# Eight gathered rows move from beside the last build to the end of the block loop

## The chip, the cores and the metric

The kernel runs on one core of one Trainium2 chip. The metric is the device time of one execution in microseconds (us), as the median of several runs. The core has five engines with their own instruction queues: PE (TensorE, matmuls), DVE (VectorE), ACT (ScalarE), POOL (GpSimd, which here issues gathers) and SP (SyncE, which here issues loads and stores). Sixteen DMA engines move the data.

## The reference, cut to what matters

One encoder layer over 512 tokens of width 1024. The part that the change touches is the feed-forward by experts (PEER): every token picks 128 of 16384 experts (8 heads, 16 each), each expert being one row of a table U and one row of a table V.

```
def one_chunk(xb):                       # 128 tokens
    ...                                  # top-k over sub-keys: idx, g  (128 experts per token)
    u = u_table[idx]
    hpre = jnp.einsum('td,ted->te', xb, u)
    act = g * jax.nn.gelu(hpre, approximate=False)
    return jnp.einsum('te,ted->td', act, v_table[idx])
...
h = layer_norm(DN_ALPHA * h + ffn + ple, ln2_g[i], ln2_b[i])
```

## The kernel before, in words

The 512 tokens are four chunks of 128. Attention, the first LayerNorm and the routing (which experts, with which weights) take the first 550 us or so. After that the experts are computed in two ways at once.

Chunk 0 is gathered. For each of its 128 picks k, `gather_u` (or `rows`, earlier on) fetches 128 rows of U, one for each token, by an indirect DMA that POOL issues (128x1024 floats, 512 KB), and DVE multiplies them with the tokens and sums (`hdot[:, k]`). After all 128, `gather_act` applies the activation, and then `gather_v` fetches the 128 rows of V for each k and DVE adds them, scaled, to `base[0]`, the sum for chunk 0. That makes 128 + 1 + 128 steps, which stand in the list `steps`.

Chunks 1 to 3 are dense. V is walked in 128 blocks of 128 experts; for each block PE multiplies a matrix of weights (`a_hi`, `a_lo`: the weights split in two parts) with the block (`hTh`/`hTl` or `whi`/`wlo`: V split in two parts) into six accumulators `acc`. The weights come from a matrix G (which expert has which routing weight for which token) times the activations `ge` of the blocks of U. G is built by `build_g` once for each of the chunks 3, 2 and 1, in that order, from one-hot matrices (`oh_i`, `oh_j` on DVE and ACT, products `tr` on PE, `g_st` out of PSUM by ACT) and kept in DRAM.

Beside these builds, under the names `pe_work`, `gate_and_leads` and `lead_block`, PE multiplies blocks of U with tokens ("leads", 108 of the 128 blocks; in the trace `mm<-whole,raw` or `hp<-whole,raw`, 16 records a block) and the results go through ACT into `ge`. `run` walks over the steps of a build and hands PE so much lead work for each (`run_pe`), and from the generator `own` it takes steps of gathered rows in proportion to a share. In the last build (chunk 1) `own` is `beside()`: it fetches the first `BESIDE` rows of U of chunk 0 and, 12 and 5 rows before its end, loads two blocks of V that it later splits (`cut`).

Then comes the loop over the 128 blocks of V (`for n, i in enumerate(order)`). In each pass DVE multiplies `gt` (G) with `ge`, splits the block (`hTl` or `wlo`) and splits the weights (`a_lo`); then some steps of chunk 0 follow: a counter `spent` grows with each pass, and `upto` says up to which step the list is worked off. The order on DVE and on SP inside the loop is that of the code; PE, ACT and POOL are ordered by the scheduler. Blocks 124 to 127 (`late`) are multiplied after the loop's last pass, accumulator by accumulator. The buffers `whi`/`wlo` are two deep, so a block there can be split only when PE is done with the block two places before.

Behind the loop stand, for each chunk, the sum with the accumulator (`fsum`), the second LayerNorm (`layer_norm`) and the store. Chunk 0 has no accumulator: it needs the last `gather_v` alone.

Of the kernel before, what the change touches and what calls it, by code (L numbers as in the profile page):

```python
# [36 lines left out]
LEAD = 108  # L37
# [4 lines left out]
PACE = 1.1  # L42
AHEAD = 14.0
LAG = 6.0
BESIDE = 26
PRE = BESIDE
OWN = 1.2
OWN_G = 0.7
OWN_G_LATE = 4.0
SEAM = 7.0  # L50
WAIT = 8.4
OWN_LATE = 10.0
LATE = 0.57
OT = 8
W_SCALE = 32768.0
G_SPLIT = 1.0
# [6 lines left out]
NO_GATHER = 1  # L63
# [16 lines left out]
def tile_encoder_layer(ctx: ExitStack, tc: tile.TileContext, A: dict, out: bass.AP):  # L80
# [995 lines left out]
    def run_pe(amount):  # L1076
        nonlocal due
        due += amount * PACE
        while due > 0:
            done = next(pe_work, 1e9)  # L1080
            due -= done
        if due < -1e6:
            due = 0.0
# [313 lines left out]
    pe_work = gate_and_leads()  # L1397
    own, own_due = None, 0.0

    def run(steps, share=0.0, n=2):  # L1400

        nonlocal own_due
        for amount in steps:
            send()
            if amount is None:
                for _ in range(n if own else 0):
                    run_pe(next(own, 0.0))
                continue
            run_pe(amount)
            own_due += amount * share  # L1410
            while own and own_due > 0:
                x = next(own, None)
                if x is None or not x:
                    own_due = -1e9
                    break
                run_pe(x)
                own_due -= x

    with tc.manual_schedule(engines={nc.vector.engine, nc.scalar.engine, nc.tensor.engine, nc.sync.engine,
# [29 lines left out]
        build = build_g(NGC, *held)  # L1449
# [1 line left out]
        run_pe(next(side))  # L1451
        own = side
        own_due = -OWN_G_LATE
        run(build, OWN_G)
        for x in own:
            run_pe(x)
        while parts:
# [88 lines left out]
    def expert_out(x, c, halves=(0, 1)):  # L1546
        n, ah, al, vh, vl = x
        cs = slice(c * 128, (c + 1) * 128)
        for i, (a, b) in enumerate(((ah, vh), (ah, vl), (al, vh))):
            for hf in halves:  # L1550
                nc.tensor.matmul(acc[c][hf], a[:, cs], b[:, hf * 512:(hf + 1) * 512],  # L1551
                                 start=(n == 0 and i == 0), stop=(n == 127 and i == 2))

    steps = list(gather_steps())
# [8 lines left out]
    with tc.manual_schedule(engines={nc.vector.engine, nc.sync.engine}):  # L1563
        for n, i in enumerate(order):
# [59 lines left out]
                expert_in(u)  # L1624
            if n >= NO_GATHER:
                spent += 1 if u else LATE
            upto = min(len(steps), PRE + math.ceil((len(steps) - PRE) * spent / (128 - (1 - LATE) * LEAD - 3 - NO_GATHER)))
            for f in steps[done:upto]:
                f()
            done = upto  # L1630
        for c in range(NDC):
            for hf in range(2):
                for x in late:
                    expert_out(x, c, (hf,))


    turned.clear()
# [100 lines left out]
```

## Time and profile before

| what | value |
|---|---|
| median of 3 runs | 1489.12 us (1486.78 to 1490.31) |
| the profiled execution, its own time | 1489.54 us |
| its span in the profile | 1487.8 us |
| PE busy | 1450.2 us, 97% of the span |
| DVE busy | 1268.5 us, 85% |
| ACT busy | 638.4 us, 43% |
| POOL busy | 570.7 us, 38% |
| mean DMA rate over the span | 305 GB/s |

The span is what the profile covers; the execution's own time has 1.7 us more around it. Busy time counts the instructions on an engine alone. Times in the views below are in us from the span's start. In a row of the timeline stand the start, the length, the engine, the line of the kernel, what is written and read, and in brackets how long the engine had waited and for whom. The third build takes from about 810 to 880 us, the loop over V from 893 to 1477 us, and the last LayerNorms end at 1484 us.

### The profile page before, as it was taken

The page shows a single profiled execution, that of the slowest core. Times are in us where ns is not written, and L with a number is a line of the kernel's source. Part 1 is how long each engine was busy: PE and PEld are TensorE (multiplying, and loading weights), DVE is VectorE, ACT ScalarE, POOL GpSimd, SP SyncE. Part 2 cuts the span into 40 slices and gives each one's busy share as a digit, 9 for nine tenths or more (in the row PEclk, how much of TensorE's full clock was granted, in tenths as well). Part 3 has the DMA queues.
Part 4 walks back from the last instruction along what each step waited for, and adds up shares of the span by engine and source line. Part 5 has one row for each costly group of instructions (what it writes and reads, how often), then busy time and mean ns, then how long its engine had stood idle before and what let it go on. Part 6 is the DMA issues. An engine that isn't in the chain of part 4 may idle for free.

```text
span 1487.8 us, 22518 instructions
## 1 busy us (share of the span) xinstructions
PE 1450.2 (97%) x7693; PEld 1212.4 (81%) x7693; DVE 1268.5 (85%) x2736; ACT 638.4 (43%) x1203; POOL 570.7 (38%) x520
## 2 busy tenths in 40 slices
PE   9999999999999999999998999999999999999997
PEld 5788777788888878888887888988888888888775
DVE  7376786579998979998776987999899999999997
ACT  3355776243221554212555763444343333333433
POOL 1013110010014544344442435665555666666630
PEclk9999999999999999999999999999999999999999
DMA  7333340175239999999999999999999999999992
GB/s 255 99 111 92 97 128 30 29 245 170 100 125 351 334 416 415 405 324 336 392 416 410 376 396 369 415 417 417 401 393 411 412 412 411 412 412 412 411 362 85
DMA packets 196851, 453.82 MB, mean 305 GB/s; under 512 B 18945, under 2 KB 96897, under 8 KB 196738
## 3 DMA queue, kind: packets, MB, share of 16 engines
q1 hardware_dynamic: 119168, 211.72, 38.6%
q0 software_dynamic: 57984, 207.12, 35.5%
q10 hardware_dynamic: 19586, 33.57, 5.9%
q8 instruction: 60, 0.98, 0.2%
q14 instruction: 53, 0.43, 0.1%
HBM read 411.70 MB, written 37.75 MB: 302 GB/s over the span
## 4 chain that ended last, share of the span: by engine, by line
PE 56%; DMA 22%; DVE 9%; issue 6%; ACT 4%; POOL 3%; SPq 0%; ACTq 0%; DVEq 0%; POOLq 0%
PE acc L1551 16%; DMA raw<-in_v_rows_dram 11%; PE mm L1291 6%; PE hp L1291 5%; DMA ge_dram<-ge 4%; PE mm L129 4%; PE mm L131 4%; PE mm L130 4%; PE pj L129 3%; PE pj L130 3%; PE pj L131 3%; DMA v_raw<-in_v_rows_dram 3%; PE hp L129 1%; PE hp L131 1%; PE hp L130 1%
## 5 line engine op out<-in xcount | busy, mean ns | idle before, releaser
L110 DVE TENSOR_TENSOR wlo<-raw,whi 128x1024 fp32r<-128x1024 f32 (+4 forms) x113 | 131.5, 1164 | 45.7 <-ACT whi L110 45.4
L110 ACT CAST a_hi<-gt 128x384 fp32r<-128x384 f32 (+2 forms) x128 | 64.9, 509 | 242.4 <-DVE gt L1598 179.5
L110 ACT CAST whi<-raw 128x1024 fp32r<-128x1024 f32 (+4 forms) x113 | 113.0, 1001 | 106.9 <-PE mm L130 47.3
L1291 PE MATMUL mm<-whole,raw 128*128 128x256 f32 x672 | 153.1, 381 | 1.5 <-DMA raw<-in_uT_dram 1.5
L1174 POOL DMA_INDIRECT whi<-in_u_rows_dram,s_ix x51 | 64.2, 1259 | 218.5 <-DVE cand L994 129.7
L1551 PE MATMUL acc<-hTh,a_hi 128*128 128x512 f32 x456 | 141.8, 391 | 0.1
L1551 PE MATMUL acc<-hTl,a_hi 128*128 128x512 f32 x456 | 141.2, 390 | 0.0
L1551 PE MATMUL acc<-hTh,a_lo 128*128 128x512 f32 x456 | 140.9, 389 | 0.0
L1291 PEld LDWEIGHTS mm<-whole,raw 128*128 128x128 f32 x672 | 125.6, 190 | 17.9 <-DMA raw<-in_uT_dram 1.9
L1534 POOL DMA_INDIRECT gat<-in_v_rows_dram,i_sel x64 | 100.8, 1574 | 55.0 <-DVE base L1536 39.5
L110 ACT CAST hTh<-v_raw 128x1024 fp32r<-128x1024 f32 x74 | 77.8, 1051 | 55.9 <-PE acc L1551 23.1
L1551 PEld LDWEIGHTS acc<-hTl,a_hi 128*128 128x128 f32 x456 | 85.4, 188 | 18.3 <-DVE hTl L110 0.4
L1551 PEld LDWEIGHTS acc<-hTh,a_lo 128*128 128x128 f32 x456 | 85.4, 188 | 18.2 <-DVE a_lo L110 0.3
L1551 PEld LDWEIGHTS acc<-hTh,a_hi 128*128 128x128 f32 x456 | 84.1, 188 | 17.2 <-ACT a_hi L110 1.1
L110 DVE TENSOR_TENSOR hTl<-v_raw,hTh 128x1024 fp32r<-128x1024 f32 x74 | 90.2, 1219 | 6.4 <-ACT hTh L110 6.4
L1551 PE MATMUL acc<-wlo,a_hi 128*128 128x512 f32 x300 | 92.8, 390 | 0.2
L1551 PE MATMUL acc<-whi,a_hi 128*128 128x512 f32 x300 | 92.8, 391 | 0.1
L1551 PE MATMUL acc<-whi,a_lo 128*128 128x512 f32 x300 | 92.6, 390 | 0.0
L1174 POOL DMA_INDIRECT wlo<-in_u_rows_dram,s_ix x51 | 61.9, 1213 | 68.3 <-DVE s_dot L1176 56.0
L1519 POOL DMA_INDIRECT gat<-in_u_rows_dram,i_sel x52 | 69.1, 1329 | 45.2 <-DVE hdot L1525 34.1
L1536 DVE SCALAR_TENSOR_TENSOR base<-gat,hdot,base 128x1024 f32<-128x1024 f32 x64 | 82.0, 1281 | 1.0
L1273 ACT ACTIVATE ge<-mm 128x256 f32<-128x256 f32 x78 | 29.6, 380 | 110.4 <-PE mm L1291 100.5
(415 smaller groups left out, 3815.7 us busy)
## 6 DMA issues: line engine op xcount, KB each, us to landing
raw<-in_uT_dram SPq DMA_DIRECT2D x80, 512.0 KB, 7.8
v_raw<-in_v_rows_dram SPq DMA_DIRECT2D x78, 512.0 KB, 13.2
raw<-in_v_rows_dram SPq DMA_DIRECT2D x48, 512.0 KB, 13.8
g_dram<-g_st ACTq DMA_DIRECT2D x40, 512.0 KB, 12.1
ge_dram<-ge ACTq DMA_DIRECT2D x96, 128.0 KB, 7.0
ge<-ge_dram SPq DMA_DIRECT2D x96, 128.0 KB, 13.0
gt<-g_dram SPq DMA_DIRECT2D x30, 384.0 KB, 13.9
raw_u<-in_uT_dram SPq DMA_DIRECT2D x19, 512.0 KB, 7.8
```

The lines of the kernel that those rows point to most:

```text
L110: cut = nc.scalar.copy(hi, src), nc.vector.tensor_tensor(lo, src, r32(hi), op=OP.subtract)
L129: nc.tensor.matmul(ps, a[0], b[0], start=start, stop=False)
L130: nc.tensor.matmul(ps, a[0], b[1], start=False, stop=False)
L131: nc.tensor.matmul(ps, a[1], b[0], start=False, stop=stop)
L1174: nc.gpsimd.indirect_dma_start(out=u[:], out_offset=None, in_=u_rows, in_offset=bass.IndirectOffsetOnAxis(ap=ix[:, k:k + 1], axis=0))
L1273: nc.scalar.activation(ge, ps[:, :N_U], AF.Gelu)
L1291: nc.tensor.matmul(ps[:, :N_U], raw[:, k], whole[:, k, :], start=(k == 0), stop=(k == 7))
L1519: nc.gpsimd.indirect_dma_start(out=u[:], out_offset=None, in_=u_rows, in_offset=bass.IndirectOffsetOnAxis(ap=i_sel[:, c, k:k + 1], axis=0))
L1534: nc.gpsimd.indirect_dma_start(out=u[:], out_offset=None, in_=v_rows, in_offset=bass.IndirectOffsetOnAxis(ap=i_sel[:, c, k:k + 1], axis=0))
L1536: nc.vector.scalar_tensor_tensor(base[c], u, hdot[:, c, k:k + 1], base[c], op0=OP.mult, op1=OP.add)
L1551: nc.tensor.matmul(acc[c][hf], a[:, cs], b[:, hf * 512:(hf + 1) * 512], start=(n == 0 and i == 0), stop=(n == 127 and i == 2))
```

## The change

`BESIDE` goes from 26 to 18: beside the last build stand 18 rows of U of chunk 0 in place of 26. The list of steps is the same, so the loop starts 8 steps further ahead in it. The pace of the loop is now worked out for all steps but the last 8 (`LAST_ROWS`), 231 steps as before; so a pass of the loop has as many rows as before, each 8 places earlier in the list, and the list is worked off but for 8 rows of V at n = 121, where before all of it was. Of those 8, one each goes into the passes n = 124 to 127, and four stand behind the loop. Two numbers for the last build change besides: the share of `own` steps (0.7 to 0.6) and 0.2 us of lead work more on PE for every step of the build (`MORE_G`).

```diff
-BESIDE = 26
+BESIDE = 18
 PRE = BESIDE
 OWN = 1.2
-OWN_G = 0.7
+OWN_G = 0.6
...
+MORE_G = 0.2
+LAST_ROWS = 8
...
-    def run(steps, share=0.0, n=2):
+    def run(steps, share=0.0, n=2, more=0.0):
...
-            run_pe(amount)
+            run_pe(amount + more)
...
-        run(build, OWN_G)
+        run(build, OWN_G, more=MORE_G)
...
-            upto = min(len(steps), PRE + math.ceil((len(steps) - PRE) * spent / (128 - (1 - LATE) * LEAD - 3 - NO_GATHER)))
+            upto = min(len(steps) - LAST_ROWS, PRE + math.ceil((len(steps) - LAST_ROWS - PRE) * spent / (128 - (1 - LATE) * LEAD - 3 - NO_GATHER)))
+            upto += max(0, n - 123)
             for f in steps[done:upto]:
                 f()
             done = upto
...
+        for f in steps[done:]:
+            f()
```

Lines of the changed kernel lie 2 further down up to the new lines in the loop and 5 further down behind them (L1536 is L1538 there, L1646 is L1651).

DVE at the end of the loop, before: the LayerNorm of chunk 0 (L138, L166 on `base`) lies among the splits of blocks 124 to 127, and behind the last split (`a_lo`) come the sums with the accumulators (L1646).

```order
L138 TENSOR_TENSOR ln_y<-ln_y 128x1
L166 SCALAR_TENSOR_TENSOR base_3028<-base_3028,ln_y,gat 128x1024
L110 TENSOR_TENSOR wlo<-v_raw,whi 128x1024
L110 TENSOR_TENSOR raw<-gt_13358,raw 128x384
L1598 TENSOR_TENSOR gt_13358<-gt_13358,ge 128x8x32
L110 TENSOR_TENSOR hTl<-v_raw,hTh 128x1024
L110 TENSOR_TENSOR a_lo<-gt_13358,a_hi 128x384
L1598 TENSOR_TENSOR gt_13358<-gt_13358,ge 128x8x32
L110 TENSOR_TENSOR hTl<-v_raw,hTh 128x1024
L110 TENSOR_TENSOR a_lo<-gt_13358,a_hi 128x384
L1646 SCALAR_TENSOR_TENSOR h_86,fsum<-acc_8458,own_top,h_86 128x512
L1646 SCALAR_TENSOR_TENSOR h_86,fsum<-acc_8459,own_top,h_86 128x512
```

The same place now, from the last split on: the last rows of V (L1538) stand between the sums with the accumulators (L1651), and the LayerNorm of chunk 0 begins behind them.

```order
L112 TENSOR_TENSOR hTl<-v_raw,hTh 128x1024
L112 TENSOR_TENSOR a_lo<-gt_13334,a_hi 128x384
L1538 SCALAR_TENSOR_TENSOR base_3028<-gat,hdot,base_3028 128x1024
L1651 SCALAR_TENSOR_TENSOR h_86,fsum<-acc_8434,own_top,h_86 128x512
L1538 SCALAR_TENSOR_TENSOR base_3028<-gat,hdot,base_3028 128x1024
L1651 SCALAR_TENSOR_TENSOR h_86,fsum<-acc_8435,own_top,h_86 128x512
L1538 SCALAR_TENSOR_TENSOR base_3028<-gat,hdot,base_3028 128x1024
L1651 SCALAR_TENSOR_TENSOR h_87,fsum<-acc_8436,h_87 128x512
L1538 SCALAR_TENSOR_TENSOR base_3028<-gat_w,hdot,base_3028 128x1024
L1651 SCALAR_TENSOR_TENSOR h_87,fsum<-acc_8437,h_87 128x512
L1538 SCALAR_TENSOR_TENSOR base_3028<-gat_w,hdot,base_3028 128x1024
L150 BN_STATS ln_st<-base_3028 128x6 x2
```

So five rows of V moved behind the last split (that of n = 127 and the four behind the loop), and chunk 0's LayerNorm moved behind all of them.

PE between the last product of the third build and the loop's first matmul (`acc`), before: 33 lead matmuls, of which the last 16 go to the PSUM tile `hp`.

```order
L1291 MATMUL mm<-whole,raw 128x256
L1291 MATMUL mm<-whole,raw_u 128x256 x8
L1291 MATMUL mm<-whole,raw 128x256 x8
L1291 MATMUL hp<-whole,raw 128x256 x16
L1551 MATMUL acc_8460<-hTh,a_hi 128x512
```

The same place now: 17 lead matmuls, 8 of them to `hp`.

```order
L1117 LDWEIGHTS oh_j
L1117 MATMUL tr<-oh_i,oh_j 128x128
L1293 MATMUL mm<-whole,raw 128x256 x9
L1293 MATMUL hp<-whole,raw 128x256 x8
L1553 MATMUL acc_8436<-hTh,a_hi 128x512
```

So 16 of the 33 lead matmuls moved from behind the build in between its products.

ACT at the same seam, before: the last `ge` out of a PSUM tile `mm` stands ahead of `whi`, the first part of the block n = 2 of V, which needs that block's load.

```order
L110 CAST hTh<-h_s 128x1024
L110 CAST a_hi<-gt_7619 128x256
L1473 COPY gt_8567<-g_st 128x256 x2
L1273 ACTIVATE ge<-mm 128x256
L110 CAST a_hi<-gt_7619 128x256
L110 CAST a_hi<-gt_7619 128x128 x2
L110 CAST whi<-v_raw 128x1024
L1273 ACTIVATE ge<-hp 128x256 x2
```

And now:

```order
L112 CAST hTh<-h_s 128x1024
L112 CAST a_hi<-gt_7619 128x128 x2
L1475 COPY gt_8543<-g_st 128x256 x2
L112 CAST whi<-v_raw 128x1024
L1275 ACTIVATE ge<-mm 128x256
L1275 ACTIVATE ge<-hp 128x256
```

The last `ge<-mm` moved behind `whi<-v_raw`.

## The prediction

> **What bounds the kernel now.** I read the table of stretches first, because the change takes work out of one stretch (the third build) and puts it into another (the end of the loop), and a share over the whole span says nothing about either. Its columns are the busy time of PE, PE's weight loads, DVE, ACT and POOL, then the granted PE clock and the DMA share.
>
> ```profile
> 815.00:828.00 13.00, 10.16 (x81) 8.68 (x81) 12.90 (x20) 11.66 (x31) 3.73 (x3) 1.00 0.82 297
> 828.00:893.40 65.40, 62.57 (x433) 55.29 (x433) 56.13 (x91) 45.20 (x110) 23.81 (x20) 0.97 1.02 403
> 893.40:1436.00 542.60, 542.37 (x2612) 456.48 (x2611) 517.26 (x693) 211.12 (x303) 333.03 (x226) 1.00 1.03 408
> 1436.00:1461.00 25.00, 24.85 (x105) 18.77 (x104) 22.91 (x36) 11.73 (x17) 0.00 (x0) 1.00 0.56 202
> 1461.00:1468.30 7.30, 7.30 (x31) 5.28 (x30) 5.57 (x8) 2.93 (x5) 0.00 (x0) 1.00 0.23 93
> 1468.30:1477.60 9.30, 9.26 (x41) 7.32 (x39) 7.83 (x24) 2.89 (x6) 0.00 (x0) 1.00 0.09 35
> 1477.60:1487.80 10.20, 0.00 (x0) 0.00 (x0) 6.01 (x19) 1.45 (x3) 0.00 (x0) 0.74 0.30 122
> ```
>
> From the third build to its last matmul the kernel lives on PE: in the loop PE is busy 542.37 of 542.60 us. DVE and the DMA engines are nearly full there too, but PE never waits for them. The number of lead matmuls and products does not change, so an earlier start of the loop can come from one source only: time that PE idles, or runs at a low clock, before it. Behind PE's last matmul 10.2 us remain, and they belong to DVE and to the last store. The end of the chain of waits (start, length, engine, what) shows the hand-over:
>
> ```profile
> 1443.46 24.82 PE acc L1551 x103
> 1468.31 2.04 DVE h L1646 x6
> ...
> 1482.54 1.28 DVE h L166
> ```
>
> DVE's last instruction ends at 1483.82; the span ends 4.0 us later, with the last store. Whatever DVE has to do more at the end shows in full, as soon as it lies behind PE.
>
> **Term 1, the build: what 8 rows fewer are worth.** Taken out are 8 indirect DMAs of 512 KB on POOL's queue and 8 multiply-and-sum instructions on DVE. Neither is on PE, so the gain is what PE waits less. First SP's issues ahead of 828, then PE's waits in the build (in brackets), with an undisturbed product (855.94) and an undisturbed pair of lead blocks (886.58) for comparison:
>
> ```profile
> 819.76 0.38 SPq L1447 DMA_DIRECT2D gt<-g_dram  x1
> 820.23 1.07 SPq L1251 DMA_DIRECT2D raw<-in_uT_dram  x2
> ```
>
> ```profile
> 827.99 1.56 PE L1291 MATMUL mm<-whole,raw 128*128 128x256 f32 x6 [1.46 <-DMA raw<-in_uT_dram]
> ...
> 855.94 1.08 PE L1115 MATMUL tr<-oh_i,oh_j 128*128 128x128 f16 x16
> 856.85 1.08 PE L1291 MATMUL mm<-whole,raw_u 128*128 128x256 f32 x4
> 859.04 1.11 PE L1115 MATMUL tr<-oh_i,oh_j 128*128 128x128 f16 x16 [1.11 <-ACT g_st L1128]
> 861.87 1.86 PE L1115 MATMUL tr<-oh_i,oh_j 128*128 128x128 f16 x16 [1.72 <-ACT g_st L1128]
> 863.53 2.05 PE L1291 MATMUL mm<-whole,raw_u 128*128 128x256 f32 x6
> ...
> 886.58 7.07 PE L1291 MATMUL hp<-whole,raw 128*128 128x256 f32 x32
> 893.29 0.81 PE L1551 MATMUL acc<-hTh,a_hi 128*128 128x512 f32 x2
> ```
>
> Up to 828 I expect no gain. PE stands there for the load of a block of U, issued at 820.23 behind a load that waited for G in DRAM. In the changed order PE has the same 27 lead matmuls and the same 3 products behind it when it needs that block, and SP's loads ahead of it have not moved: PE arrives earlier and waits longer. The 2.84 us of idle time in the stretch before (13.00 less 10.16) stay.
>
> From 828 to 893.40 PE idles 65.40 - 62.57 = 2.83 us, which is the two waits of 1.11 and 1.72. The clock of 0.97 costs another 0.03 x 65.4 = 2.0 us; one sees it in the product at 861.87, which takes 1.66 us up to the next row where the one at 855.94 takes 0.91. So 4.8 us is the most there is to win. Those two waits come where two products follow each other with hardly any lead work between (the code holds 7 us of leads back for the seam, `SEAM`), and ACT is late with `g_st`. In the changed order this place exists as well, with 5 lead matmuls ahead of the pair and 3 behind, and ACT has as much to do. But elsewhere a product now has about 8 lead matmuls with it (each is two records; 16 records are 3.36 us by the row at 886.58, which has 32 in 6.71), so DVE and ACT, with fewer rows to share with, come to the pair with more of a lead. I take half of 4.8, rounded: **-2.5 us**. The ends: all of it (-4.8), or a loss of 1.5 if the seam opens (rival C).
>
> The 16 lead matmuls that moved ahead cost nothing in themselves; what hides the seam is the 17 that are left, about 17 x 2 x 0.21 = 7.1 us.
>
> **Term 2, the loop up to n = 121.** The pace is the same 231 steps over the same passes, so POOL issues and DVE works as much per pass as before; eight rows of U stand there in place of eight of V. Both engines keep their slack against PE (517.26 of 542.60 on DVE). Zero, and the cover is PE; if PE started more than a few microseconds ahead of the loads, DMA at 1.03 would be late next.
>
> **Term 3, the end: eight rows of V more on DVE.** A row of V takes 1.19 us from its start to the next instruction's. The rows that matter on DVE at the end, and the matmuls that hold it:
>
> ```profile
> 1434.85 1.28 DVE L1536 SCALAR_TENSOR_TENSOR base<-gat,hdot,base 128x1024 f32<-128x1024 f32 x1
> 1436.04 0.41 DVE L1598 TENSOR_TENSOR gt<-gt,ge 128x256 f32<-128x256 f32 x1
> ...
> 1451.38 0.69 DVE L148 BATCH_NORM_STATS2 ln_st<-base 128x6 f32<-128x512 f32 x1
> ...
> 1453.91 0.69 DVE L148 BATCH_NORM_STATS2 ln_st<-base 128x6 f32<-128x512 f32 x1
> 1454.64 0.21 DVE L149 BATCH_NORM_AGGREGATE ln_mu<-ln_st 128x2 f32<-128x12 f32 x1
> ...
> 1454.95 1.27 DVE L163 SCALAR_TENSOR_TENSOR base<-base,ln_mu,gat 128x1024 f32<-128x1024 f32 x1
> ...
> 1459.60 1.29 DVE L166 SCALAR_TENSOR_TENSOR base<-base,ln_y,gat 128x1024 f32<-128x1024 f32 x1
> 1461.98 1.23 DVE L110 TENSOR_TENSOR wlo<-v_raw,whi 128x1024 fp32r<-128x1024 f32 x1 [1.09 <-ACT whi L110]
> ...
> 1468.31 0.75 DVE L1646 SCALAR_TENSOR_TENSOR h<-acc,own_top,h 128x512 f32<-128x512 f32 x1 [0.75 <-PE acc L1551]
> ...
> 1471.97 0.15 DVE L158 TENSOR_SCALAR ln_y<-ln_y 128x1 f32<-128x1 f32 x1 [1.36 <-ACT gat_w L157]
> ```
>
> ```profile
> 1460.11 0.62 PE L1551 MATMUL acc<-whi,a_lo 128*128 128x512 f32 x2
> ...
> 1477.17 0.39 PE L1551 MATMUL acc<-hTh,a_lo 128*128 128x512 f32 x1
> ```
>
> ```profile
> 1459.95 1.05 ACT L110 CAST hTh<-v_raw 128x1024 fp32r<-128x1024 f32 x1
> 1460.90 1.05 ACT L110 CAST whi<-v_raw 128x1024 fp32r<-128x1024 f32 x1
> ```
>
> The anchor is 1461.98: DVE's split of block 125. It cannot come earlier against PE, since ACT's `whi` takes the buffer that PE frees with the last matmul of block 123 (1460.11). Before the change, LayerNorm of chunk 0 fills DVE's time in front of that anchor. Now it cannot, since `base` still lacks seven rows at this point: the row of n = 124 fits in, and then DVE waits some 4 us with nothing to do (4.3 for that LayerNorm, worked out below, plus the 1.09 it waits today, less 1.19). All the rest comes behind the anchor:
>
> - seven rows of V (n = 125, 126, 127 and the four): 7 x 1.19 = 8.3 us;
> - LayerNorm of chunk 0: 0.69 + 0.69 + 0.21 + 1.27 + 1.29 = 4.2 us and seven instructions of about 0.15 on one column, less some 0.08 of overlap each: 4.3 us;
> - less what DVE idles behind the anchor today and can fill: 0.75 + 1.36 = 2.1 us, and a little between the dependent small steps of the last LayerNorms, about 0.2.
>
> 8.3 + 4.3 - 2.3 = **+10.3 us**, from 1483.82 to about 1494. PE ends at 1477.6 and does not cover it: in DVE's order the six sums with the accumulators stand between the last rows and behind them. The store behind it keeps its 4.0 us. The ends: 9 (more small gaps filled) and 11.5 (waits for the activations of ACT in the tail, which now come close to each other). The gathers themselves are hidden: their buffers are freed at the latest by the row that is the last today, and a gather lands within about 8 us:
>
> ```profile
> 1448.72 1.28 DVE L1536 SCALAR_TENSOR_TENSOR base<-gat_w,hdot,base 128x1024 f32<-128x1024 f32 x1
> ```
>
> ```profile
> gat<-in_v_rows_dram,i_sel POOLq DMA_INDIRECT x64, 8.1
> ```
>
> **Sum.** 1489.5 - 2.5 + 0 + 10.3 = 1497.3 us against the profiled execution; the median of the runs shown lies 0.4 lower, so 1497 (+0.5%). Two runs differ by up to 0.2% (1486.78 to 1490.31), about what a measurement of this kernel can tell from no change.
>
> **Rivals.**
>
> A, faster: the eight rows cost nothing at the end, since DVE gets through them while PE still multiplies 16.6 us (1460.6 to 1477.2). Then only term 1 is left: 1489 - 2.5 to -4.8, about 1485.5. For it: DVE is idle there at times. Against it: it would need 12.6 us of idle DVE time behind the anchor to take the seven rows and the LayerNorm, and there are 2.3; it decides in the moment that DVE finishes the fourth row before 1470. Chance 0.05.
>
> B, no change: the build is held by the DMA engines and not by ACT. They are at 1.02 there with 403 GB/s; 8 x 524,288 bytes are 4.2 MB, or 10.4 us at that rate, more than everything PE loses. Then all waits go, the ones ahead of 828 too: 2.84 + 4.8 = 7.6, and 1489.1 - 7.6 + 10.3 = 1491.8. For it: ACT's own queue waits for its stores in this stage. Against it: the wait at 828 is for a load that is issued late, at a DMA share of 0.82. [...] Chance 0.09.
>
> C, slower still: the seam opens. The first `acc` matmul takes the PSUM tile that the last `ge<-mm` frees, and this now stands behind `whi<-v_raw` in ACT's order.
>
> ```profile
> 880.54 1.52 SPq L1489 DMA_DIRECT2D v_raw<-in_v_rows_dram  x3
> ...
> 890.92 1.05 ACT L110 CAST whi<-v_raw 128x1024 fp32r<-128x1024 f32 x1 [2.18 <-DMA v_raw<-in_v_rows_dram]
> ```
>
> The block landed 10.4 us after its issue; `whi` and `ge` take 1.4 more, and PE has 7.1 us of leads behind the last product. If the load is issued when the last product ends, PE waits 10.4 + 1.4 - 7.1 = 4.7 us. But the load now waits for DVE's last row only, which DVE can reach some 4 us before PE's last product, so I expect a wait of 0 to 1. With 4.7 lost and 2.5 won, the time is 1489.1 + 2.2 + 10.3 = 1501.6. A pause of this length has a second price, which the trace shows at 861.87, where 2.8 us of waits bring the clock to 0.97 over the stretch. [...] Chance 0.18.
>
> That the change does not do what it says is excluded by the order of the instructions.
>
> **How the numbers follow.** The forecast as summed has 0.68, C 0.18, B 0.09, A 0.05. The likeliest gives 1497, with its own range from 1493.3 (9 - 4.8) to 1500 (11.5, -0.5). Out to 1501.5 it takes in C; down to 1492.5 the edge towards B. Slower by over 0.2% (above 1492.1): the forecast and C, 0.86. Within 0.2%: B, 0.09. Faster: A, 0.05.
>
> **What the profile afterwards would show.** Right: DVE waits 3 to 5 us ahead of block 125's split, then is busy without a gap for 32 us, the LayerNorm of chunk 0 lies behind PE's last matmul, and from that matmul to the end of the span are about 20 us in place of 10.2. The first `acc` comes at 889 to 892 in place of 893.3, and PE stands at about 828 longer than 1.46. Wrong: `acc` earlier than 888 (B), or `base` normalised before the last matmul (A), or a wait of the first `acc` for ACT (C).

## The result, and the profile after

| | median | runs |
|---|---|---|
| before | 1487.95 us | 6 (1486.19 to 1493.84) |
| after | 1497.07 us | 6 (1495.71 to 1498.07) |

The ratio is 1.0055, with a 95% interval from 1.0037 to 1.0074: slower by about half a per cent. The profiled execution of the changed kernel took 1496.71 us, with a span of 1494.7; the one of before took 1489.54 with 1487.8.

Four instants cut the span into stages: the starts of PE's first transposition of the third build (`tr<-ident,e1s`), of the first `acc` and of the last `acc`, and the end of DVE's last instruction. Their rows in the timeline (start, length, engine); first the one of before that the prediction has not shown, then those of after:

```profile
809.75 0.27 PE L1090 MATMUL tr<-ident,e1s 128*128 128x128 f32 x1
```

```profile
811.26 0.27 PE L1092 MATMUL tr<-ident,e1s 128*128 128x128 f32 x1
890.97 0.81 PE L1553 MATMUL acc<-hTh,a_hi 128*128 128x512 f32 x2
1474.34 0.39 PE L1553 MATMUL acc<-hTh,a_lo 128*128 128x512 f32 x1
1489.50 1.28 DVE L168 SCALAR_TENSOR_TENSOR h<-h,ln_y,gat 128x1024 f32<-128x1024 f32 x1
```

| stage | before | after | difference |
|---|---|---|---|
| up to the third build | 809.75 | 811.26 | +1.51 |
| build, to the first `acc` | 83.54 | 79.71 | -3.83 |
| loop, to the last `acc` | 583.88 | 583.37 | -0.51 |
| tail, to DVE's end | 6.65 | 16.44 | +9.79 |
| last store | 3.98 | 3.92 | -0.06 |
| span | 1487.8 | 1494.7 | +6.9 |

So the tail costs 9.8 us, and the build wins some of it back. The 1.51 us ahead of the build lie where the change touches nothing; in the profiles of the experiments below that instant lay anywhere from 808.36 to 811.73, so it is what two executions differ by.

The stretches of after, cut at the matching places (busy time of PE, PE's weight loads, DVE, ACT, POOL; then the granted clock, the DMA share and GB/s):

```profile
815.00:828.00 13.00, 13.00 (x95) 11.24 (x95) 11.65 (x19) 10.35 (x26) 2.30 (x2) 1.00 0.86 319
828.00:891.00 63.00, 60.81 (x427) 53.81 (x425) 47.61 (x77) 46.45 (x113) 15.61 (x13) 0.97 0.89 342
891.00:1433.70 542.70, 542.70 (x2619) 458.44 (x2618) 517.98 (x703) 210.45 (x303) 337.45 (x229) 1.00 1.03 409
1433.70:1458.20 24.50, 23.19 (x99) 17.45 (x98) 19.07 (x24) 10.49 (x15) 8.09 (x5) 1.00 0.86 328
1465.50:1474.70 9.20, 9.20 (x41) 7.21 (x39) 9.20 (x16) 1.80 (x2) 0.00 (x0) 1.00 0.32 114
1474.70:1494.70 20.00, 0.03 (x1) 0.00 (x0) 15.87 (x46) 4.32 (x10) 0.00 (x0) 0.62 0.26 105
```

Behind PE's last matmul lie 20.0 us in place of 10.2, and DVE is busy in 15.87 of them. From 1465.5 to 1474.7 DVE is busy all the time (9.20 of 9.20), where before it had gaps.

The tail on DVE, in order (in brackets the wait and for whom):

```profile
1454.52 0.41 DVE L1600 TENSOR_TENSOR gt<-gt,ge 128x256 f32<-128x256 f32 x1
1459.25 1.23 DVE L112 TENSOR_TENSOR wlo<-v_raw,whi 128x1024 fp32r<-128x1024 f32 x1 [4.33 <-ACT whi L112]
1460.40 0.55 DVE L112 TENSOR_TENSOR raw<-gt,raw 128x384 fp32r<-128x384 f32 x1
1460.87 1.28 DVE L1538 SCALAR_TENSOR_TENSOR base<-gat_v,hdot,base 128x1024 f32<-128x1024 f32 x1
...
1467.14 1.28 DVE L1538 SCALAR_TENSOR_TENSOR base<-gat,hdot,base 128x1024 f32<-128x1024 f32 x1
1468.33 0.74 DVE L1651 SCALAR_TENSOR_TENSOR h<-acc,own_top,h 128x512 f32<-128x512 f32 x1
...
1474.49 1.27 DVE L1538 SCALAR_TENSOR_TENSOR base<-gat_w,hdot,base 128x1024 f32<-128x1024 f32 x1
1475.79 1.29 DVE L150 BATCH_NORM_STATS2 ln_st<-base 128x6 f32<-128x512 f32 x2
```

DVE waits 4.33 us ahead of the split of block 125, and then works off seven rows, the sums and four LayerNorms. The LayerNorm of chunk 0 begins at 1475.79, behind PE's last matmul. From that split to DVE's end it is 1490.78 - 1459.25 = 31.53 us; before, it was 1483.82 - 1461.98 = 21.84.

PE in the build has one wait left in this execution, at two products with no lead work in between, and the clock is low there (0.50 from 841.3 to 844.7; 16 products take 1.66 us up to the next row, where the undisturbed ones of the prediction's rows take 0.91):

```profile
838.25 1.08 PE L1117 MATMUL tr<-oh_i,oh_j 128*128 128x128 f16 x16
841.52 1.86 PE L1117 MATMUL tr<-oh_i,oh_j 128*128 128x128 f16 x16 [2.19 <-ACT g_st L1130]
843.18 1.16 PE L1293 MATMUL mm<-whole,raw_u 128*128 128x256 f32 x2
```

### The profile page after: what moved, and what is told of

Same layout as the page of the kernel before. It is cut to its first block, busy times and chain, and to the rows that moved or that the text cites. A ratio compares the mean times of both kernels' runs of the same rounds, so it can differ in the third digit from the quotient of the medians.

```text
span 1494.7 us, 22522 instructions
## 1 busy us (share of the span) xinstructions
PE 1451.2 (97%) x7693; PEld 1215.7 (81%) x7693; DVE 1268.5 (85%) x2736; ACT 638.7 (43%) x1203; POOL 570.6 (38%) x520
## 4 chain that ended last, share of the span: by engine, by line
PE 74%; DMA 10%; DVE 8%; ACT 3%; issue 3%; POOL 1%; ACTq 0%; DVEq 0%; POOLq 0%; SPq 0%
PE acc L1553 28%; PE mm L1293 10%; PE hp L1293 5%; DMA ge_dram<-ge 5%; PE mm L131 4%; PE mm L133 4%; PE mm L132 4%; DMA ge<-ge_dram 4%; PE pj L131 3%; PE pj L132 3%; PE pj L133 3%; PE tr L1117 2%; PE hp L131 1%; PE hp L133 1%; PE hp L132 1%
## 5 line engine op out<-in xcount | busy, mean ns | idle before, releaser
L1293 PE MATMUL mm<-whole,raw 128*128 128x256 f32 x688 | 156.6, 381 | 0.0
L1293 PEld LDWEIGHTS mm<-whole,raw 128*128 128x128 f32 x688 | 129.1, 191 | 17.0 <-DMA raw<-in_uT_dram 0.3
L1536 POOL DMA_INDIRECT gat<-in_v_rows_dram,i_sel x64 | 101.9, 1593 | 59.7 <-DVE base L1538 45.1
L1521 POOL DMA_INDIRECT gat<-in_u_rows_dram,i_sel x56 | 74.4, 1329 | 51.0 <-DVE hdot L1527 40.6
L1538 DVE SCALAR_TENSOR_TENSOR base<-gat,hdot,base 128x1024 f32<-128x1024 f32 x64 | 81.9, 1280 | 0.9
L112 DVE TENSOR_TENSOR a_lo<-gt,a_hi 128x384 fp32r<-128x384 f32 (+2 forms) x128 | 69.6, 544 | 10.3 <-ACT a_hi L112 9.9
## 6 DMA issues: line engine op xcount, KB each, us to landing
g_dram<-g_st ACTq DMA_DIRECT2D x40, 512.0 KB, 12.6
```

Of the source, the lines that this page charges most:

```text
L112: cut = nc.scalar.copy(hi, src), nc.vector.tensor_tensor(lo, src, r32(hi), op=OP.subtract)
L1293: nc.tensor.matmul(ps[:, :N_U], raw[:, k], whole[:, k, :], start=(k == 0), stop=(k == 7))
L1521: nc.gpsimd.indirect_dma_start(out=u[:], out_offset=None, in_=u_rows, in_offset=bass.IndirectOffsetOnAxis(ap=i_sel[:, c, k:k + 1], axis=0))
L1536: nc.gpsimd.indirect_dma_start(out=u[:], out_offset=None, in_=v_rows, in_offset=bass.IndirectOffsetOnAxis(ap=i_sel[:, c, k:k + 1], axis=0))
L1538: nc.vector.scalar_tensor_tensor(base[c], u, hdot[:, c, k:k + 1], base[c], op0=OP.mult, op1=OP.add)
```

## The experiments

Every kernel is told by its difference from the changed kernel. The medians of the kernel before differed a little from one set of runs to the next (1487.95 to 1489.99 us), so each ratio is against the runs of before in the same set. The stages come from one profiled execution of each kernel, cut at the four instants above:

| kernel | median, us | ratio to before (95%) | build | loop | tail |
|---|---|---|---|---|---|
| before | | | 83.54 | 583.88 | 6.65 |
| after | 1497.07 | 1.0055 (1.0037 to 1.0074) | 79.71 | 583.37 | 16.44 |
| e1 build only | 1494.76 | 1.0049 (1.0036 to 1.0062) | 80.01 | 592.41 | 6.63 |
| e2 end only | 1495.75 | 1.0048 (1.0032 to 1.0065) | 81.25 | 580.64 | 16.38 |
| e3 held rows sooner | 1490.83 | 1.0011 (0.9999 to 1.0023) | 80.47 | 586.08 | 7.85 |
| e4 fewer rows only | 1501.06 | 1.0085 (1.0072 to 1.0098) | 86.80 | 584.41 | 16.40 |
| e6 leads only | 1491.95 | 1.0026 (1.0012 to 1.0040) | 79.50 | 590.42 | 6.64 |
| e7 eight not gathered | 1488.14 | 0.9989 (0.9977 to 1.0000) | 81.23 | 584.31 | 6.64 |
| e8 eight not added | 1495.19 | 1.0038 (1.0023 to 1.0054) | 81.04 | 591.77 | 6.63 |
| e9 leads, three held | 1492.89 | 1.0025 (1.0015 to 1.0035) | 79.68 | 589.27 | 6.64 |
| e10 leads and share | 1491.67 | 1.0012 (1.0000 to 1.0024) | 82.46 | 583.68 | 6.62 |
| e11 two rows more | 1487.29 | 0.9985 (0.9973 to 0.9997) | 84.14 | 580.65 | 6.65 |
| e12 last four out | 1491.22 | 1.0014 (1.0001 to 1.0026) | 81.93 | 583.58 | 11.64 |
| e13 seam seven | 1485.45 | 0.9975 (0.9963 to 0.9987) | 79.58 | 581.20 | 6.63 |

The table also says how far one execution can be trusted. The build of after, e1, e3, e7, e8 and e12 is in the same order of code and took 79.7 to 81.9 us; that of before and e2 took 83.5 and 81.3. A difference of 2 us in the build of one execution is not yet an effect. The tail repeats within 0.1 us (6.62 to 6.65; 16.38 to 16.44). Nor is a profiled execution always a middle one: that of e4 took 2.9 us more than the median of its kernel and that of e12 2.3 more, that of e10 2.8 less.

### The two halves apart (e1, e2)

```diff
 e1: the rows are spread over the pace of the loop
-LAST_ROWS = 8
+LAST_ROWS = 0
...
-            upto += max(0, n - 123)
```

> The half of the change at the build alone: 18 rows of U beside the third build with 0.6 and 0.2 as in the changed kernel, but no row held back; the eight rows are spread over the loop's pace up to n = 121 (239 steps in place of 231), and the end is as in the kernel before. Theory (the build gives 2 to 4 us, the tail on DVE costs all the rest, and the loop hides rows under PE, since DVE was busy 517.26 of 542.60 us there and eight rows are 9.5): first acc at 889 to 891.5, PE without a wait in the loop, DVE's end about 6 us behind PE's last matmul as before, 1485.5 us (1484.5 to 1487). Rival (the loop has no room either, because its DMA share is 1.03 at 408 GB/s, and eight gathers more before n = 121 are 4.2 MB or 10.3 us at that rate): PE waits in the loop for its blocks or for DVE's splits, 1490 to 1496 us.

The theory on the loop fell here, and the time lies in the rival's range. The tail came as expected and the first `acc` at 888.37, 0.6 us ahead of the range, but the loop took 8.5 us more: 1494.76 us, about as slow as the whole change.

```diff
 e2: the build as before
-BESIDE = 18
+BESIDE = 26
-OWN_G = 0.6
+OWN_G = 0.7
-MORE_G = 0.2
+MORE_G = 0.0
```

> The half of the change at the end alone: 26 rows beside the build with 0.7 and 0.0 as before, and the last eight rows of V held back as in the changed kernel (the loop's pace is then 223 steps). Theory: first acc at 893 as before, DVE's wait of about 4 us ahead of block 125's split, 31.5 us from that split to DVE's end in place of 21.8, so +9.7 and no gain: 1497.6 us (1496.5 to 1499). If the two halves add up, this run less the kernel before and the build half less the kernel before together give the 9.1 us of the whole change. Rival (the slower pace gives the loop time back, DMA at 1.03 there): PE's last matmul 3 us or more sooner than the start of the loop explains, 1490 to 1494 us.

The tail costs 9.73 us, as expected. But the rival's mechanism is there as well: the loop, with 223 steps in place of 231, took 3.2 us less, and the median of 1495.75 lies between the two ranges. Set side by side, the places at which the six accumulators pass from one block to the next run apart between before and e2 at two places above all: by 1.6 us at 475 to 490 us into the loop, and by 1.1 at 545 to 557. The matmuls of the kernel before start a little later there one by one. PE's busy share does not show it, but the waits of PE's weight loads (PEld) do. In before, from 900 to 1450 (what waited for whom: us in total, times, longest):

```profile
PEld acc L1551 <- ACT a_hi L110: 2.2, 5, 0.5
PEld acc L1551 <- DVE wlo L110: 1.7, 5, 0.6
PEld acc L1551 <- DVE a_lo L110: 1.2, 7, 0.2
PEld acc L1551 <- DVE hTl L110: 0.4, 2, 0.2
```

That is 5.5 us in all; in e2 there is none. The first of the late places shows where it comes from, a block of V that lands late at ACT:

```profile
1370.62 1.05 ACT L110 CAST whi<-raw 128x1024 fp32r<-128x1024 f32 x1 [3.51 <-DMA raw<-in_v_rows_dram]
1372.13 0.30 PEld L1551 LDWEIGHTS acc<-whi,a_hi 128*128 128x128 f32 x2 [0.53 <-ACT a_hi L110]
```

By the medians the two halves cost 5.8 and 6.8 us, 12.6 together, and the whole change 9.1 (by the ratios it is 0.97% against 0.55%). In the profiled executions the surplus lies in the loop: +8.5 in e1 and -3.2 in e2, against -0.5 with both together, where the loop has as many rows as before.

### What is full in the loop (e7, e8)

Both are e1 with one resource relieved. In e7, 8 of the 128 rows of V are not gathered; in e8, they are gathered but not added.

```diff
 e7, in gather_v
-        u = gat()
-        nc.gpsimd.indirect_dma_start(out=u[:], ...)
+        if k % 16 != 8:
+            u = last_u = gat()
+            nc.gpsimd.indirect_dma_start(out=u[:], ...)
+        u = last_u
 e8, in gather_v
-        nc.vector.scalar_tensor_tensor(base[c], u, hdot[:, c, k:k + 1], base[c], op0=OP.mult, op1=OP.add)
+        if k % 16 != 8:
+            nc.vector.scalar_tensor_tensor(base[c], u, hdot[:, c, k:k + 1], base[c], op0=OP.mult, op1=OP.add)
```

> The build half once more (239 steps of pace), but 8 of the 128 rows of V (every sixteenth) are not gathered; DVE adds the row before them once more, so its work is the same and the DMA engines have 4.2 MB, 10.3 us at 408 GB/s, less. Compared with the build half (1494.76 us, 592.4 us from first acc to the last). Theory D (the DMA engines are what is full in the loop): the waits for a_hi behind whi behind a block of V go, the loop takes 581 to 585 us, 1484.5 to 1487.5 us. Theory E (DVE is what is full): the loop keeps most of its 8.5 us of waits, 1492 to 1495 us.

> The counterpart: the same 8 rows of V are gathered but not added, so the DMA engines have all their bytes and DVE 8 x 1.19 = 9.5 us less. Theory D (DMA full): the loop keeps most of its waits, 590 us or more from first acc to the last, 1492 to 1495 us. Theory E (DVE full, and the block loads late only since SP's issues wait for buffers that DVE frees): 581 to 585 us and 1484.5 to 1487.5 us. Both runs between these: the two are full together.

Theory D holds in the main, on both sides: 4.2 MB less in the DMA engines give the loop back 8.1 us (592.41 to 584.31), 9.5 us less on DVE give 0.6. The medians missed theory D's ranges by little (1488.14 us for at most 1487.5, 1495.19 for at most 1495). The table of stretches from 893 to 1436 shows it in one row each, first e7, then e8:

```profile
893.00:1436.00 543.00, 543.00 (x2608) 453.56 (x2607) 526.16 (x710) 210.14 (x303) 337.17 (x226) 1.00 1.03 410
```

```profile
893.00:1436.00 543.00, 537.95 (x2579) 448.31 (x2578) 511.95 (x697) 209.28 (x301) 334.28 (x233) 1.00 1.03 410
```

The DMA share is 1.03 in both, with 410 GB/s, and over the same stretch it is 1.03 with 408 to 411 GB/s in before, after, e10, e11, e12 and e13 as well: it does not tell the loop of e11 (580.65 us) from that of e8 (591.77). ACT is the first to need each block of V. Its waits from 1170 to 1436 (what waited for whom: us in total, times, longest), for before, after, e1, e8, e2 and e7:

```profile
ACT whi L110 <- DMA raw<-in_v_rows_dram: 22.2, 13, 5.1
ACT hTh L110 <- DMA v_raw<-in_v_rows_dram: 12.2, 11, 2.6
```

```profile
ACT whi L112 <- DMA raw<-in_v_rows_dram: 19.3, 10, 4.5
ACT hTh L112 <- DMA v_raw<-in_v_rows_dram: 7.2, 9, 2.6
```

```profile
ACT whi L112 <- DMA raw<-in_v_rows_dram: 23.4, 9, 6.9
ACT hTh L112 <- DMA v_raw<-in_v_rows_dram: 9.7, 8, 2.3
```

```profile
ACT whi L112 <- DMA raw<-in_v_rows_dram: 26.2, 9, 7.3
ACT hTh L112 <- DMA v_raw<-in_v_rows_dram: 18.6, 9, 5.8
```

```profile
ACT a_hi L112 <- PE acc L1553: 114.1, 48, 2.7
ACT a_hi L112 <- DVE gt L1600: 50.5, 17, 3.0
```

```profile
ACT a_hi L112 <- DVE gt L1604: 147.5, 56, 3.0
ACT a_hi L112 <- issue: 17.4, 8, 2.2
```

In e2 and e7, ACT waits for no block in this stretch. In before it does so 24 times, mostly without harm, since it works about one block ahead of PE (the `whi` made at 1384.36 is first used at 1389.76); in e1 the longest wait is 6.9 us, and PE behind it stands for 2.97 us at `a_hi`, with slow matmuls after that (a pair takes 0.85 us at 1309.51 and 1310.36, and 0.45 from 1311.92 on). The sum of these waits does not rank the kernels: e13 has 20.1 us of them here, and its PE is hardly late.

What ranks them is how late PE is. Taken at the same matmul, 556 us into the loop of e2, and counted from the first `acc` (in e6 and e9 from behind the pause at the start of the loop), PE is not late or at most 0.2 us late against e2 with 228 and 229 steps (e9, e11, e13), 2.7 to 3.8 with 231 (before, after, e4, e6, e10, e12), and 10.8 to 10.9 with 239 (e1, e8). The sum of the waits of PE's weight loads from 900 to 1450 goes the same way: at most 0.6 us, 4.4 to 6.0, and 15.7 to 16.3. So the bend lies at about 229 steps, and from there to 239 a step costs about 1.1 us.

Two things stay open. e7 takes 8 issues from POOL and 8 turns of a gather buffer as well as the bytes, and no run parts these; POOL was busy for 337 of 543 us. And e7 is still 3.7 us above the loop of e2 although ACT waits for no block from 1170 on. Its PE is 3.0 us late by the same matmul, with 8.8 us of waits of the weight loads; DVE, busy for 526.16 of 543.00 us, is the likely next limit, which no run tests.

### Which part of the build's change wins (e4, e6)

```diff
 e4: no other spread of the lead work
-OWN_G = 0.6
+OWN_G = 0.7
-MORE_G = 0.2
+MORE_G = 0.0
```

> The changed kernel with the share at 0.7 and the additional lead work at 0.0 as before: eight rows fewer beside the build and the rows at the end, but no other spread of the lead matmuls (38 of them stand behind the last product in place of 17). Theory A (the gain in the build comes from the lead work that stands in between the products): the waits for the block of U near 816 to 828 and for g_st come back, first acc at 892 to 894, 1498.5 to 1500 us. Theory B (it comes from DVE and DMA having eight rows less to do): first acc at 890 to 891.5, no wait for the block of U, 1496.5 to 1498 us.

Theory A was right in direction and too small in size: without the spread the build of the profiled execution takes 86.80 us, 3.3 more than before. This execution was 2.9 us above the median of its kernel; by the medians e4 is 4.0 us slower than the changed kernel, with intervals that only just overlap. Every row brings its own share of lead work with it (`run_pe(x)`), so with eight rows fewer and nothing in their place there is less lead work between the products. PE's waits in this build:

```profile
PE tr L1117 <- ACT g_st L1130: 5.4, 3, 2.4
PE tr L1117 <- DVE oh_j L1158: 1.8, 5, 0.5
PE mm L1293 <- DMA raw<-in_uT_dram: 1.1, 1, 1.1
PE tr L1117 <- ACT oh_i L1151: 1.1, 1, 1.1
```

They come to 9.4 us. In the profile of the changed kernel one is left, 2.2 us for `g_st`; the five other executions with the same build have 2.9 to 5.1 us of waits, before 5.7 and e2 4.7.

```diff
 e6: the spread of the lead work alone, no row moved
-BESIDE = 18
+BESIDE = 26
-LAST_ROWS = 8
+LAST_ROWS = 0
...
-            upto += max(0, n - 123)
```

> No row moved: 26 rows beside the build and the end as before, with only the two numbers of the build changed (share 0.6, 0.2 us more lead work for each step), so that 17 lead matmuls stand behind the last product in place of 33. Theory A (the build gains from the spread of the lead work): from its first products to the first acc about 80 us as in the changed kernel in place of 83.5, the loop as before (583.9 us), the tail 6.65 us: 1486 us (1484.5 to 1487.5), faster than both kernels. Theory B (eight rows fewer are needed as well, since the build of the end half alone took 81.3 us with the leads as before, so that some 2.3 us are no more than differences between executions): 1488 to 1489.5 us; or, if the seam opens for want of leads, 1490 us and more.

The build was as short as theory A says, and the seam gave it back, as the last clause of theory B has it. Here the smaller share pushes rows to the end of the build, 17 lead matmuls are too few to cover them, and PE stands after its first four `acc`: DVE's last row waits 3.69 us for its gather, and `a_lo` stands behind it.

```profile
891.68 1.23 DVE L1178 CUSTOM_DVE_ANT_0 whi<-whi,h 128x1024 f32<-128x1024 f32 x1 [3.69 <-DMA whi<-in_u_rows_dram,i_sel]
892.83 0.42 DVE L112 TENSOR_TENSOR a_lo<-gt,a_hi 128x256 fp32r<-128x256 f32 x1
```

```profile
889.02 0.62 PE L1553 MATMUL acc<-hTl,a_hi 128*128 128x512 f32 x2
893.30 1.22 PE L1553 MATMUL acc<-hTh,a_lo 128*128 128x512 f32 x2 [3.66 <-issue]
...
898.59 1.00 PE L1553 MATMUL acc<-hTh,a_lo 128*128 128x512 f32 x2
899.43 0.62 PE L1553 MATMUL acc<-hTh,a_hi 128*128 128x512 f32 x2
```

From 893.30 to 899.43, PE runs 14 matmuls in 6.13 us, where 14 x 0.227 = 3.2 us would do (a pair takes 0.455 in the rows behind, and 0.85 from 894.32 on): the pause of 3.66 cost another 2.9. So the spread needs either fewer rows or a larger share.

### What costs in the tail (e3, e12)

```diff
 e3: the eight held rows in the passes 117 to 124
-            upto += max(0, n - 123)
+            upto += max(0, min(LAST_ROWS, n - 116))
```

> The changed kernel with the same eight rows held back up to n = 116 and then one row more in each of the passes 117 to 124; none stands behind the split of block 125. Theory (what costs is what DVE has behind the split of block 125, seven rows and the LayerNorm of chunk 0): the seven rows (8.3 us) go from the tail, the wait of 4.33 us ahead of the split is filled, most of the LayerNorm (about 3.5 us) stays behind PE; 1488 us (1486.5 to 1489.5). Rival (DVE has no time for eight rows in those passes either; 9.5 us of rows against 4.3 us of idle time, so it comes late with the splits and PE waits about 5 us): 1491 to 1494 us, with waits of PE for wlo or a_lo at 1425 to 1465.

1490.83 us lies between the two. The tail is as the theory has it (7.85 us, 8.6 less than after for seven rows less). But the rival is half right: 2.7 us more than in after went into the loop, with two waits of PE for `a_hi` of 1.4 and 1.3 us that end at 1442.27 and 1448.00. There `a_hi` waits for `gt`, which stands behind rows of V on DVE, and DVE is busy for 9.93 of the 10 us from 1440 to 1450.

```diff
 e12: without the four rows behind the loop
-        for f in steps[done:]:
-            f()
```

> The changed kernel without the four rows of V behind the loop: they are neither gathered nor added. It prices a row in the tail. Theory (DVE works without a gap from the split of block 125 to its end, so each row there shows in full): 4 x 1.19 = 4.8 us less than the changed kernel, tail 11.5 to 12 us in place of 16.44, 1492.3 us (1491 to 1493.5). Rival (part of the tail is waits for the accumulators or for ACT that open again when the rows go): 3.5 us less or even nearer, 1493.5 to 1495 us.

The tail went from 16.44 to 11.64 us, 4.80 or 1.20 for each row: a row there shows in full. The median went down by 5.85 us, more than expected by one microsecond, which is within what two medians differ by here.

### Versions (e9, e10, e11, e13)

```diff
 e9: e6, and three rows held out of the pace, one more in each of the passes 121 to 123
-LAST_ROWS = 8
+LAST_ROWS = 3
...
-            upto += max(0, n - 123)
+            upto += max(0, min(LAST_ROWS, n - 120))
```

> Like the run with the spread lead work alone, and three rows of V held out of the loop's pace (228 steps), one more in each of the passes n = 121, 122 and 123, so that the LayerNorm of chunk 0 stays ahead of the split of block 125. Theory (the loop of the kernel before loses 2.8 us to waits that are gone with eight rows fewer, and three rows at the end find room on DVE): 1 to 2 us less than the run with the lead work alone, tail 6.6 to 7.2 us, 1484 to 1486 us. Rival (DVE has no room in these passes, as with eight rows held back): waits of PE for a_hi at 1435 to 1465, no gain or up to 2 us more than the run with the lead work alone.

The rival: no gain. The 2.8 us of the theory were indeed gone up to 556 us into the loop, but the seam opens as in e6 (4.40 us), and PE waits 0.96 and 1.05 us for the splits of late blocks (up to 1464.28 and 1466.76). The tail stays at 6.64, since LayerNorm of chunk 0 is again ahead of the split.

In e10, e11 and e13 no row is held (`LAST_ROWS = 0`, without the line with `n - 123`); they differ in four numbers of the build (here written in one line each):

```diff
-BESIDE, OWN_G, MORE_G, SEAM = 18, 0.6, 0.2, 7.0
 e10
+BESIDE, OWN_G, MORE_G, SEAM = 26, 0.75, 0.1, 9.0
...
 e11
+BESIDE, OWN_G, MORE_G, SEAM = 28, 0.75, 0.05, 8.0
...
 e13
+BESIDE, OWN_G, MORE_G, SEAM = 28, 0.75, 0.05, 7.0
```

> No row moved, 26 rows beside the build, the lead work spread by 0.1 us for each step, with the share at 0.75 and 9 us held back for the seam: 22 lead matmuls stand behind the last product, and 3 rows of U stand on DVE between its last one-hot and the first a_lo, where the run with 0.6 and 0.2 had 17 and 8 and PE stood 3.66 us at the seam. Theory (that pause came from rows that the smaller share had pushed to the end, and the spread of the leads is worth 2 to 3 us by itself): build 80 to 81.5 us, no wait at the seam, loop 583 to 585 us, tail 6.65 us, 1487 us (1485.5 to 1488.5), faster than both kernels or equal to the one before. Rival (with 26 rows the build is held by its DMA, and what the leads win there is lost at the seam or in the loop): 1489 to 1492 us.

The seam is closed (no wait there), so the larger share does what it should. But the build took 82.46 us in this execution and the median says no gain: 1.0012, the rival. Where the median lost is not shown, as the profiled execution was 2.8 us below it.

> Two rows more beside the build than in the kernel before (28; share 0.75, 0.05 us, 8 us for the seam: 26 lead matmuls behind the last product, 5 rows ahead of the first a_lo), so that the loop has 229 steps in place of 231. Theory (the DMA engines are full in the loop, and each gather more or less there moves its end: 592.4 us at 239 steps, 583.4 to 583.9 at 231, 580.6 at 223): loop 582.5 to 583.5 us, build 81 to 83 us, 1487 us (1485.5 to 1489). Rival (the build's DMA engines are as full, at 1.03 from 830 to 860, so two rows more cost there what they save in the loop, 1.3 us each or more): 1489 to 1492 us.

Faster than before, if only just: 0.9985, the interval ends at 0.9997. The two rows fewer in the loop are worth 3.2 us there, as much as eight fewer in e2: below 229 steps nothing more was to be had in these executions. The build lost some of it, at two products close together:

```profile
866.24 0.27 PE L1117 MATMUL tr<-oh_i,oh_j 128*128 128x128 f16 x1 [1.72 <-ACT g_st L1130]
867.41 1.78 PE L1117 MATMUL tr<-oh_i,oh_j 128*128 128x128 f16 x15 [0.90 <-DVE oh_j L1158]
868.99 4.37 PE L1293 MATMUL mm<-whole,raw 128*128 128x256 f32 x10
```

The ten lead records at 868.99 take 4.2 us up to the next matmul (873.19), twice what they take at full clock (32 in 6.71).

> The run with 28 rows beside the build, with 7 us in place of 8 held back for the seam: 23 lead matmuls behind the last product in place of 26, and one lead or two more at the place where products follow each other closely (there PE waited 1.72 and 0.90 us, and the clock was 0.88 from 860 to 888). Theory (this pause and the slow clock behind it are what the build lost against the 80 us of the changed kernel; loop and tail as before, 580.7 and 6.65 us): build 81 to 83 us in place of 84.1, 1485.5 us (1484 to 1487). Rival (the pause only moves, since ACT is late with g_st wherever two products stand together): build 83.5 to 85 us, 1486.5 to 1488.5 us.

1485.45 us, ratio 0.9975 (0.9963 to 0.9987): faster than both kernels. The pair of waits is still there, as the rival said, but no slow clock follows, and the build is shorter than the theory's range:

```profile
865.47 0.22 PE L1117 MATMUL tr<-oh_i,oh_j 128*128 128x128 f16 x1 [1.72 <-ACT g_st L1130]
866.38 1.04 PE L1117 MATMUL tr<-oh_i,oh_j 128*128 128x128 f16 x15 [0.70 <-DVE oh_j L1158]
```

From 860 to 888, e11 and then e13:

```profile
860.00:888.00 28.00, 25.16 (x173) 21.84 (x172) 23.09 (x37) 18.84 (x46) 12.60 (x11) 0.88 0.96 373
```

```profile
860.00:888.00 28.00, 25.36 (x186) 22.28 (x186) 24.34 (x40) 19.82 (x48) 12.62 (x11) 1.00 0.98 395
```

The larger part of the difference between e11 and e13 in the build (84.14 and 79.58) is thus this clock: 0.12 of 28 us is 3.4 of the 4.6. That the 7 us held back kept it away is not shown, since the pair of waits is nearly the same and one execution of each was profiled. The medians lie 1.84 us apart, and the intervals of the two ratios overlap.

## Why the prediction was right, point by point

**The end (+10.3): right, 0.5 too large.** The anchor, the rows and the order were as written: seven rows behind the split, the LayerNorm of chunk 0 behind PE, 4.33 us of waiting ahead of the split (3 to 5 were said). From the split to DVE's end it is 31.53 - 21.84 = +9.69, and DVE's end against PE's +9.79. The term that was mis-sized is the idle time that the new work can fill: 8.3 + 4.3 - 9.7 = 2.9 us in place of 2.3. e12 gives 1.20 us for a row where 1.19 was taken.

**The sum: its closeness is luck.** 1497 was said and 1497.07 measured, but the profiled executions differ by 6.9 us in span where the terms gave 7.8. The build won 1.3 more than said, the tail cost 0.5 less, the loop took 0.5 less and the stages ahead of the build 1.5 more. By the medians the change costs 9.1 us, since three more runs put the median of before at 1487.95 in place of 1489.12.

**The build (-2.5): the size fits, the reasoning only in part.** In the profiled execution the stage became 3.83 us shorter, and the 1.51 us of the stages ahead of it, which the change does not touch, left -2.3 at the first `acc` (890.97; 889 to 892 were said). Over the six executions with the changed build and the two with the old one, the means are 80.7 and 82.4, so -1.7: of the forecast's size, and with this scatter not to be told from 2.5. What failed is the step "up to 828 I expect no gain", with PE standing there longer than 1.46: in the changed kernel's profile there was no wait at all (13.00 of 13.00 busy). The other five executions of this build had one of 1.2 to 1.9 us, so the place is as the prediction saw it and the wait comes and goes; that its price was fixed was wrong. The load that PE waits for there was issued 8.4 us after the build's first instant in the changed kernel's profile, 9.7 to 11.2 in those five and 10.5 in before. So the time of this issue, which the prediction took as unmoved, does move. The reason given, that DVE and ACT come with more of a lead since they have fewer rows, did not carry it alone either: by e4, fewer rows without the spread make the build longer (by 3.3 us in its profiled execution). The other half of that sentence, that a product now has more lead work with it, did. The pair of products in the middle kept its wait (2.19), as said.

**The loop (0): right by its number, with one reason that holds and one that does not.** "The pace is the same 231 steps" holds: 583.88 and 583.37 us are alike because the number of steps is the same. "Both engines keep their slack against PE", with PE as the cover, is what the runs refute. Eight steps more cost 8.5 us and eight fewer gained 3.2, since above about 229 steps the loads and gathers come late (e7, e8). In the changed kernel the same 2.8 us are lost, at another place: 0.2 up to 540 us into the loop and 2.6 from there to 556, where before had lost 1.7 by 490. PE's busy time of 542.37 of 542.60 hid this: matmuls that start a little late count as busy there, and "PE never waits" was not so, by the 5.5 us of waits of PE's weight loads. The prediction named DMA at 1.03 as what would be late next, but put it a few microseconds away; it was there already.

**The rivals.** A (the rows hidden under PE) did not come about: rows behind the split show at 1.20 us each. Ahead of it most of their time is hidden, but DVE has no room for all eight there (e3: 7.85 us of tail, and 2.7 more in the loop). B (the build held by the DMA engines) did not decide the build's time, but its mechanism rules the stage next to it, where 408 to 411 GB/s were moved from 893 to 1436 us in before, after, e7, e8 and e10 to e13. The most that the DMA engines can move is not shown (e10 has 417 GB/s from 830 to 860). C did not come about in the changed kernel: `whi` ran at 887.00 and PE went from the last lead matmul into `acc` with no wait. The seam did open in e6 and e9, though by another chain, the late row on DVE ahead of `a_lo`, so that its pauses of 3.66 and 4.40 us lie near the 4.7 that C gave is luck.

## What to carry to other kernels

Before work is moved between stages, ask of each stage whether it can take one piece more and what one piece fewer would give. Near the point where a second resource fills up, the price up and down is not the same (here +8.5 and -3.2 us for eight rows), and a term is zero only as long as the number stays. When the busy engine is at 100% and the DMA share too (here 542.37 of 542.60 us and 1.03), neither share says how much is left; look at the waits of PE's weight loads (5.5 us in before, none in e2), and compare the start of the same matmul in two kernels. At the end of a kernel, find the last instruction that another engine holds. What stood behind it in the same queue showed in full here (1.20 us for a row in e12); work ahead of it was hidden as far as its data could be there and the engine had room (in e3 the tail is 8.6 us shorter than in after, and the loop 2.7 longer).

## What the runs showed of the hardware

A low clock came with some pauses of 1.7 to 4.4 us, and not with others. In the clock records of before and after the granted clock is 1.00 or 0.50, and from 812 us to the end of the loop the half rate comes once in each, for 3.41 us: the clock is 0.50 from 861.2 to 864.6 in before and from 841.3 to 844.7 in after. In the changed kernel a wait of 2.19 us was enough for 16 products to take 1.66 us in place of 0.91.

In the other kernels the mean clock and the rows show losses of that size. By the clock (0.08 of 18 us and 0.01 of 30 in e8, 0.06 of 28 in e10) it is 1.7 us, which is one such stretch, and in e11 (0.12 of 28) 3.4, which is two. In e6 the matmuls behind a pause of 3.66 us were slow for 6.13 us, a pair taking 0.85 us in place of 0.455; the pauses of 2.97 in e1 and 4.40 in e9 also have pairs of 0.85 us behind them.

The length of a wait does not settle whether a stretch follows. Waits of 1.79 us (e8, all that PE idles from 812 to 830) and 2.19 brought one, while e4 had waits of up to 2.4 us with a clock of 1.00 in each of the stretches 812 to 830, 830 to 860 and 860 to 888, and behind the 3.07 of e8 at 1309.53 the pairs took 0.45 to 0.47 us from 1310.94 to 1313.71. Nor does it help to look at pairs: 1.11 and 1.72 in before and 1.72 and 0.90 in e11 brought the half rate, 1.72 and 0.70 in e13 did not. What decides it, no run here shows. So beyond itself a short wait cost nothing, or what PE loses in one or two such stretches (1.7 us in e8, 2.9 in e6, 3.4 in e11).
